# A tile of eight gate-norm weights that takes 64 bytes per partition in place of 32

## The chip, the cores and the metric

The kernel runs on one NeuronCore of one Trainium2 chip. The metric is the device time of one execution in microseconds (us). Matrix products run on TensorE (PE in the profile, its loads of stationary operands PEld), elementwise work on VectorE (DVE) and ScalarE (ACT), a little on GpSimd (POOL). All bulk transfers are issued from SyncE's queue (SPq).

## The reference

One block over 2048 tokens of width 1024, in float32, cut to what matters here:

```python
n = rms_norm(h, attn_norm)
z = n @ w_in                        # columns for two groups of heads
o_g = gated linear attention of 4 heads, chunked, from z
o_m = softmax attention of 8 heads with a block-causal mask, from z
h = h + concat(o_g, o_m) @ w_out
m = rms_norm(h, mlp_norm)
h = h + square(relu(m @ w_mlp_up)) @ w_mlp_down          # 1024 -> 4096 -> 1024
gate = sigmoid(rms_norm(h, ple_norm) @ w_ple_gate + b_ple_gate)
h = h + (p @ w_ple_proj) * gate
```

The result has to agree with float32 products, so every matrix product here is made of three passes over rounded parts.

## The kernel before

**Three passes.** `split` (lines 89 to 96) writes an operand as a high part (ACT, line 92 or 95) and a low part (DVE, line 93 or 96), both of the type fp32r. `mm3` (lines 98 to 101) multiplies high by high, high by low and low by high into one PSUM tile. Its first argument is the stationary operand, its second the moving one. The first two passes have the same stationary operand, yet each matmul comes with a weight load of its own.

**Stages.** First the projections, with gated linear attention and the preparation of the softmax heads woven in (lines 544 to 716). Then attention, head by head (lines 730 to 906). Then, in two halves `H` of 1024 tokens each, the out projection, the MLP and the gate, called the tail here (lines 908 to 1034).

**The tail.** Its weights come in tiles `w2_` of [128, 2, 512] fp32r: `wtile2` loads 128x512 float32 into `raw2` and splits it. `wr_` holds 12 such tiles, `rw` four `raw2`. The activations lie in `xT` (two buffers of [128, 2, 8, 512]) or in `a` (five of [128, 2, 512]). All products of the tail have a moving operand of 512 columns and a stationary one of 128x128:

- out projection (line 955): 2 halves x 2 column halves x 8 token tiles x 8 depth blocks x 3 = 768 matmuls, stationary `xT`, moving `w2_`;
- MLP up (line 983): 2 x 16 groups of 256 features x 4 x 8 x 3 = 3072, stationary `w2_`, moving `xT`;
- MLP down (line 997): 2 x 16 x 8 x 4 x 3 = 3072, stationary `a`, moving `w2_`;
- gate and its partner product (lines 1023 and 1027): 2 x 2 x 8 x (8 + 2) x 3 = 960, stationary `xT` or `a`, moving `w2_`.

Between them stand groups of transposes: `rows_T` normalizes 128 rows, and PE turns them (line 921, 32 calls of eight transposes in two groups of four); line 1011 turns `p` (16 pairs).

**The projections' counterpart.** In the first stage the weights are tiles `w`, the normalized rows `nT0` and `nT1`. Most products there move `w` (256, 304 or 320 columns) past a stationary `nT`; the GLA queries and keys (line 667 on) move 512 columns of `nT` past a stationary `w`.

**Where tiles lie.** Pools hand out bytes of each partition one after another, a tile in whole units of 32 bytes; pools marked `side="right"` grow from the other end. On the left, after the constants, stand `cc` (`gain_m` of 4096 bytes, `gain_p` of 32, `bias_p` of 4096, in this order), then `rw`, then `wr_`. Start addresses in the built program, in bytes of a partition:

| tile | start before | start after | mod 64 before | mod 64 after |
|---|---|---|---|---|
| `gain_p` | 22944 | 22944 | 32 | 32 |
| `bias_p` | 22976 | 23008 | 0 | 32 |
| `raw2` (4 buffers) | 27072 + 2048 i | 27104 + 2048 i | 0 | 32 |
| `w2_` (12 buffers) | 35264 + 4096 i | 35296 + 4096 i | 0 | 32 |
| `xT` (2) | 163808 + 32768 i | same | 32 | 32 |
| `a` (5) | 110560 + 4096 i | same | 32 | 32 |
| `w` (9, projections) | 163296 + 2560 i | same | 32 | 32 |
| `nT0`, `nT1` | 186336, 202720 | same | 32 | 32 |
| `kT` (2), `qT` (4), attention | 163552 + 16384 i, 212960 + 4096 i | same | 32 | 32 |

The slices that matmuls take of these tiles start at multiples of 64 bytes within them, low parts included. (`vv`, the values of attention, is the exception: its blocks are 520 bytes apart.) So the last columns hold for every operand of a product.

**Order.** Each engine works through its instructions in the order of the text; the tile framework adds the waits.

Of the kernel before, what the change touches and what calls it, by code (L numbers as in the profile page):

```python
# [11 lines left out]
F32 = mybir.dt.float32  # L12
# [10 lines left out]
P = 128  # L23
# [6 lines left out]
PLE = 256  # L30
# [18 lines left out]
def hymba_block(ctx, tc, x, p, positions, attn_norm, w_in, gla_gate_w2, gla_gate_b,  # L49
# [7 lines left out]
    x, p, out = x[0], p[0, 0], out[0]  # L57
# [31 lines left out]
    def split(hi, lo, src, gain=None):  # L89
        """src (times a gain per partition) as a sum of two numbers of 12 bits each."""  # L90
        if gain is None:
            A.copy(out=hi, in_=src)  # L92
            V.tensor_tensor(out=lo, in0=src, in1=hi, op=ALU.subtract)  # L93
        else:
            A.activation(hi, src, AF.Copy, scale=gain)  # L95
            V.scalar_tensor_tensor(out=lo, in0=src, scalar=gain, in1=hi, op0=ALU.mult, op1=ALU.subtract)  # L96
# [6 lines left out]
    def rstd_of(ss, n, shape):  # L103
        """(ss / n + eps) ** -0.5: a first guess from the exponent bits, then Newton."""
        v = small.tile(shape, F32, name="rs_v")
        V.tensor_scalar(out=v, in0=ss, scalar1=1.0 / n, scalar2=EPS, op0=ALU.mult, op1=ALU.add)
        y = small.tile(shape, F32, name="rs_y")
        A.activation(y, v.bitcast(I32), AF.Exp, bias=y0_b, scale=Y0_S)
        for _ in range(3):
            a = small.tile(shape, F32, name="rs_a")  # L110
            V.tensor_tensor(out=a, in0=y, in1=y, op=ALU.mult)  # L111
            V.scalar_tensor_tensor(out=a, in0=a, scalar=-0.5, in1=v, op0=ALU.mult, op1=ALU.mult)  # L112
            r = small.tile(shape, F32, name="rs_y")
            V.scalar_tensor_tensor(out=r, in0=a, scalar=1.5, in1=y, op0=ALU.add, op1=ALU.mult)
            y = r
        return y
# [12 lines left out]

    def gain_cols(pool, name, vec, n):  # L130
        g = pool.tile([P, n], F32, name=name)
        for k in range(n):
            dma(out=g[:, k:k + 1], in_=vec[k * P:(k + 1) * P].unsqueeze(1))
        return g

    # ================================================= projections, GLA, MLA heads
    pgl = ExitStack()
# [60 lines left out]
    rows = tmp([4, P], "rows")  # L198
# [46 lines left out]
    def rope_tables():  # L245
# [7 lines left out]
        for i in range(NF):  # L253
            f = float(np.float32(np.float64(THETA) ** (-(2.0 * i) / ROPE)))
            V.tensor_scalar(out=ang[:, :, i], in0=pos, scalar1=f, scalar2=None, op0=ALU.mult)
        # angles brought into [-pi, pi]: 2 pi in three parts
        MAGIC = 12582912.0
# [30 lines left out]

    # operands whose zeros stay: scores, queries and states kept apart by head
    st8, xq8, sz = [], [], []  # L290
# [18 lines left out]
    def later(f, n):  # L309
        """Run f when n more pieces have come."""  # L310
        if f is not None:
            rest.append(f)
        while len(rest) > n:
            rest.pop(0)()

    LL, LC, EB, DP = 1, 1, 2, 3

    # ---- GLA of one half block (two chunks of 128 tokens), in pieces
    def gla_pieces(u, tok0, gq, gk, bt, gvs, gss):
# [73 lines left out]
        def chunk(c):  # L393
# [15 lines left out]
            for g in range(2):  # L409
                for j in range(2):  # L410
                    js = slice(j * 64, j * 64 + 64)
                    V.scalar_tensor_tensor(out=new[js, g, j], in0=state[js, g, j], scalar=eb[js, g, c, P - 1:P],
                                           in1=pk[js, g], op0=ALU.mult, op1=ALU.add)
            # output norm and gate
            ss = small.tile([P, GH], F32, name="oss")
# [22 lines left out]

    # ---- MLA heads of one token tile, four heads at a time
    def mla_weights(c):  # L440
# [13 lines left out]
    def mla_tile(b, tt, c, wts, cT, krr, kss, rt, rc):  # L454
# [8 lines left out]
        for k in range(2):  # L463
# [6 lines left out]
        V.tensor_scalar(out=ssq[:, 0], in0=ssq[:, 0], scalar1=rc[:, 1, 0, tt:tt + 1], scalar2=None, op0=ALU.mult)  # L470
        # rotation of the query, its gains in the tables
        qa = ml.tile([P, 4, ROPE], F32, name="qa", bufs=1)
# [23 lines left out]
                        in1=rc[:, 0, :, tt:tt + 1].broadcast_to([P, 2, 4]), op=ALU.mult)  # L496
        # the gains of both sides go to the query
        for hh in range(4):
# [21 lines left out]

    pend = []          # pieces of the GLA of the block before
    mla_q = []         # token tiles of MLA heads

# [6 lines left out]

    stores = []        # their last parts, one tile behind

# [11 lines left out]
    for b in range(NB):  # L544
        # ---- normalized rows, transposed: two tiles of four feature blocks
        nT = [nTp.tile([P, 2, 4, BLK], F32R, name=f"nT{i}") for i in range(2)]
# [17 lines left out]
        if b == 0:  # L564
            rope_tables()
            gain_columns()
        # ---- c_q | g_low | k_r, token-major
        rt = []
# [15 lines left out]
        for tt in range(4):  # L584
# [11 lines left out]
            A.activation(sq[:, 0:ROPE], kr, AF.Square, accum_out=kss[:, tt:tt + 1])  # L596
            # rotary part of the shared key, its gains in the tables
            ra = small.tile([P, ROPE], F32, name="kra")
# [12 lines left out]

        # ---- log decays and their running sums in the chunks
        bts = []
# [19 lines left out]
        if b == 0:  # L633
            level_masks()
        # ---- c_kv and GLA values, token-major
        gvs = []
        wy = wtiles([(O_C + QR, KVR), (O_GV, 192)])
        for tt in range(4):
# [14 lines left out]
            drain(DY)  # L653
        # the norms of c_q and c_kv, left for the heads: r and r * r
        rc = ml.tile([P, 2, 2, 4], F32, name="rc")
# [9 lines left out]

        # ---- GLA queries and keys, feature-major
        gqk = []
# [17 lines left out]

        # ---- rest of the GLA values, token-major
        wz = wtiles([(O_GV + 192, 320)])
# [8 lines left out]

        # ---- GLA output gates, token-major: silu without its factor 1/2
        gss.extend(gin.tile([P, 2, GH * GV], F32, name="gs", bufs=GSB) for _ in range(2))
# [31 lines left out]

    # ================================================= attention, head by head
    pat = ExitStack()
# [11 lines left out]
    def shift_pieces(h, jb, kT):  # L744
        """The rows' maxima over their keys, negated, as one more row of the queries."""
        qT = ah.tile([QK + 1, 2, BLK], F32R, name="qT", bufs=4)
# [36 lines left out]
    def attend(h, jb, kT, vv, qT):  # L783
        npair = 2 * jb + 2
        # the blocks on the diagonal come first
        order = [npair - 2, npair - 1] + list(range(npair - 2))
# [59 lines left out]

    LOOK = 3           # pairs of key blocks whose scores run ahead
    AHEAD = 3          # steps whose maxima run ahead
    steps = [(h, jb) for h in range(MH) for jb in range(4)]
# [57 lines left out]

    # ================================================= out projection, MLP, PLE
    pcr = ctx.enter_context(ExitStack())
# [14 lines left out]
    for H in range(2):  # L924
        t0 = H * 1024
        # ---- h = x + mix @ w_out
        mix, hts = [], []
        for c in range(2):
            if c == 1 and H == 1:
                w_first = wout(0)  # L930
            m = xTp.tile([P, 2, 8, BLK], F32R, name="xT")
            for k in range(8):
                raw = rw.tile([P, 512], F32, name="raw2")
                dma(out=raw, in_=mixd[k, :, t0 + c * BLK:t0 + (c + 1) * BLK])
                split(m[:, 0, k], m[:, 1, k], raw)
            mix.append(m)
            if c == 0 and H == 0:
                gain_m = cc.tile([P, D], F32, name="gain_m")
                dma(out=gain_m, in_=mlp_norm[0].partition_broadcast(P))
                gain_p = gain_cols(cc, "gain_p", ple_norm[0], 8)  # L940
                bias_p = cc.tile([P, D], F32, name="bias_p")
                dma(out=bias_p, in_=b_ple_gate[0].partition_broadcast(P))
            for tt in range(c * 4, c * 4 + 4):
                ht = hp.tile([P, D], F32, name="h")
                dma(out=ht, in_=x[t0 + tt * P:t0 + (tt + 1) * P, :])
                hts.append(ht)
        for nh in range(2):
            ns = slice(nh * 512, (nh + 1) * 512)
            w = w_first if nh == 0 else wout(nh)
            for tt in range(8):  # L950
                ts_ = slice((tt % 4) * P, (tt % 4 + 1) * P)
                ps = ps_mm()
                m = mix[tt // 4]
                for k in range(8):
                    mm3(ps, (m[:, 0, k, ts_], m[:, 1, k, ts_]), (w[k][:, 0], w[k][:, 1]), k == 0, k == 7)
                V.tensor_tensor(out=hts[tt][:, ns], in0=ps, in1=hts[tt][:, ns], op=ALU.add)
                # the first rows' norms run beside the products of the others
                if nh == 1 and tt >= 4:
                    if tt == 4:
                        mT = [xTp.tile([P, 2, 8, BLK], F32R, name="xT")]  # L960
                    rows_T(hts[tt - 4], gain_m, mT[0], slice((tt - 4) * P, (tt - 3) * P))
        # ---- MLP
        mT.append(xTp.tile([P, 2, 8, BLK], F32R, name="xT"))
        late = [(hts[tt], gain_m, mT[1], slice((tt - 4) * P, (tt - 3) * P)) for tt in range(4, 8)]
        rT = []
        for fg in range(FF // 256):
# [24 lines left out]
            for tt in range(8):  # L991
# [8 lines left out]
                if fg == FF // 256 - 1:  # L1000
                    if tt % 4 == 0:
                        rT.append(xTp.tile([P, 2, 8, BLK], F32R, name="xT"))
                    rows_T(hts[tt], None, rT[tt // 4], slice((tt % 4) * P, (tt % 4 + 1) * P))
        # ---- PLE
        pT = [ap_.tile([P, 2, 512], F32R, name="a").rearrange("p l (k t) -> p l k t", k=2) for _ in range(4)]
# [58 lines left out]
```

## Time and profile before

| | |
|---|---|
| device time, median of 3 runs | 3169.53 us (3169.33 to 3169.77) |
| span of the profiled execution, first to last instruction | 3163.8 us |
| PE busy | 3037.9 us, 96% |
| PE loads of stationary operands | 2453.2 us, 78% |
| DVE busy | 1958.0 us, 62% |
| ACT busy | 1251.1 us, 40% |
| share of the DMA engines, main queue | 25.6% |

The profile gives the span of its execution and no other time of it; 5.7 us lie between that span and the median of the timed runs. The stages by the trace: projections to about 720 us, attention to 1268 us, the tail to the end.

Matmuls are pipelined: a row of the timeline gives the start of each and a modelled end, which overlaps the next start. The pace of a row of matmuls is therefore read from start to start, never from a mean duration. PEclk is the granted clock as a share of full speed (1.00 is the 2.4 GHz level, 0.5 the 1.2 GHz level). The trace leaves one trailing underscore out of a tile's name and keeps its number: `w__20209` is a buffer of `w2_`.

### The profile page before, as it was taken

Reading aid. Unit: us, or ns where it says so; the run is one execution under the profiler, and the core shown is the slowest. Engines: PE = TensorE matmul, PEld = TensorE weight load, DVE = VectorE, ACT = ScalarE, POOL = GpSimd, SP = SyncE. Lnnn points to the kernel's source line nnn. Section 1 sums busy time; section 2 is a strip of 40 time slices with the busy share of each in tenths; the row PEclk is TensorE's granted clock in tenths of the full one; section 3 lists DMA queues with packets and bytes.
Section 4 is the critical chain, followed back from the end, with each engine's and each line's share of the span. In section 5 each row is a group of like instructions: output and inputs, shape, how many; then the busy total and the mean of one; then the engine's idle time right before and its main releaser. Section 6 shows DMA issues by size and latency. Waiting matters only on the chain.

```text
span 3163.8 us, 41322 instructions
## 1 busy us (share of the span) xinstructions
PE 3037.9 (96%) x14851; PEld 2453.2 (78%) x14851; DVE 1958.0 (62%) x4389; ACT 1251.1 (40%) x2540; POOL 203.2 (6%) x408
## 2 busy tenths in 40 slices
PE   7899898979999999999999999999999999999999
PEld 6888887766677777778888888878878888888877
DVE  6979898887887886464444444464464444444463
ACT  7566665634666667332221222142232222212231
POOL 3322322220000000000000000000000000000000
PEclk9999999987999999999999999999999999999999
DMA  4535344361423220411111111114211111111111
GB/s 122 147 87 156 103 131 123 95 163 44 124 67 101 68 67 14 148 53 41 53 50 45 50 44 54 40 54 149 91 54 54 41 54 40 54 40 54 41 51 52
DMA packets 222525, 238.77 MB, mean 75 GB/s; under 512 B 26630, under 2 KB 174160, under 8 KB 220528
## 3 DMA queue, kind: packets, MB, share of 16 engines
q1 hardware_dynamic: 222000, 236.01, 25.6%
q8 instruction: 117, 1.92, 0.2%
q14 instruction: 88, 0.72, 0.1%
q0 software_dynamic: 320, 0.13, 0.0%
HBM read 185.60 MB, written 50.46 MB: 75 GB/s over the span
## 4 chain that ended last, share of the span: by engine, by line
PE 78%; DVE 13%; ACT 4%; issue 3%; DMA 1%; POOL 0%; SPq 0%; DVEq 0%; ACTq 0%; POOLq 0%
PE mm L101 11%; PE mm L100 11%; PE mm L99 11%; PE big L99 10%; PE big L100 9%; PE big L101 9%; PE mm L823 5%; PE tp L758 2%; PE big L797 2%; PE big L799 2%; PE big L798 2%; DVE w L96 2%; DVE rs_a L112 1%; DVE rs_a L111 1%; DVE qn L499 1%
## 5 line engine op out<-in xcount | busy, mean ns | idle before, releaser
L999 DVE TENSOR_TENSOR h<-big,h 128x1024 f32<-128x1024 f32 x256 | 313.2, 1223 | 280.8 <-PE big L101 279.7
L823 PE MATMUL mm<-ph,vv 128*66 128x512 f32 (+3 forms) x960 | 244.6, 368 | 2.9 <-ACT ph L92 2.2
L99 PE MATMUL mm<-w,nT 128*128 128x320 f32 (+2 forms) x640 | 204.4, 320 | 5.6 <-ACT w L95 2.6
L100 PE MATMUL mm<-w,nT 128*128 128x320 f32 (+2 forms) x640 | 199.5, 313 | 5.8 <-DVE w L96 5.3
L93 DVE TENSOR_TENSOR ph<-pe,ph 128x1024 fp32r<-128x1024 f32 (+4 forms) x224 | 176.6, 797 | 38.4 <-ACT ph L92 36.8
L101 PE MATMUL mm<-w,nT 128*128 128x320 f32 (+2 forms) x640 | 198.4, 311 | 1.7 <-DVE nT L93 1.7
L765 DVE TENSOR_REDUCE mx<-tp 128x1 f32<-128x512 f32 (+2 forms) x288 | 169.9, 607 | 15.4 <-PE tp L758 13.5
L823 PEld LDWEIGHTS mm<-ph,vv 128*66 128x66 f32 (+1 forms) x960 | 127.3, 139 | 55.5 <-ACT ph L92 3.2
L92 ACT CAST ph<-pe 128x1024 fp32r<-128x1024 f32 (+4 forms) x224 | 156.2, 712 | 28.7 <-PE mm L823 25.9
L99 PEld LDWEIGHTS mm<-w,nT 128*128 128x128 f32 x640 | 126.6, 198 | 11.0 <-ACT w L95 4.9
L100 PEld LDWEIGHTS mm<-w,nT 128*128 128x128 f32 x640 | 126.5, 198 | 9.1 <-DVE w L96 8.9
L758 PE MATMUL tp<-kT,qT 96*128 96x512 f32 (+2 forms) x320 | 128.1, 407 | 4.2 <-DVE mx L765 2.3
L101 PEld LDWEIGHTS mm<-w,nT 128*128 128x128 f32 x640 | 126.3, 197 | 4.3 <-DVE nT L93 2.4
L96 DVE SCALAR_TENSOR_TENSOR w<-raw,gain_a,w 128x256 fp32r<-128x256 f32 (+2 forms) x224 | 119.0, 544 | 10.0 <-ACT w L95 9.3
L797 PE MATMUL big<-qT,kT 97*128 97x512 f32 (+1 forms) x320 | 122.7, 383 | 1.2 <-ACT qT L778 0.3
L95 ACT ACTIVATE w<-raw,gain_a 128x256 fp32r<-128x256 f32 (+2 forms) x224 | 110.7, 533 | 29.7 <-DMA raw<-in_w_in_dram 14.6
L798 PE MATMUL big<-qT,kT 96*128 96x512 f32 (+1 forms) x320 | 120.3, 376 | 0.0
L799 PE MATMUL big<-qT,kT 96*128 96x512 f32 (+1 forms) x320 | 119.9, 375 | 0.0
L804 ACT ACTIVATE pe<-big 128x1024 f32<-128x1024 f32 x96 | 98.2, 1023 | 28.1 <-PE big L799 27.2
L758 PEld LDWEIGHTS tp<-kT,qT 96*128 96x128 f32 x320 | 62.4, 196 | 36.3 <-DVE mx L765 12.8
L810 ACT ACTIVATE pe<-big 128x512 f32<-128x512 f32 (+3 forms) x128 | 54.3, 436 | 67.4 <-DVE big L809 60.4
L1029 DVE TENSOR_TENSOR sg<-big,bias_p 128x512 f32<-128x512 f32 x32 | 22.1, 690 | 89.7 <-PE big L101 89.7
(3372 smaller groups left out, 8258.6 us busy)
## 6 DMA issues: line engine op xcount, KB each, us to landing
raw<-in_w_mlp_up_dram SPq DMA_DIRECT2D x128, 256.0 KB, 2.9
raw<-in_w_mlp_down_dram SPq DMA_DIRECT2D x128, 256.0 KB, 3.2
raw<-in_w_in_dram SPq DMA_DIRECT2D x160, 128.0 KB, 2.5
qd<-qko SPq DMA_DIRECT2D x64, 192.0 KB, 2.7
kd<-qko SPq DMA_DIRECT2D x64, 192.0 KB, 3.1
kT<-kd SPq DMA_DIRECT2D x8, 1536.0 KB, 11.6
qT<-qd SPq DMA_DIRECT2D x32, 384.0 KB, 4.3
vd<-vt SPq DMA_DIRECT2D x32, 260.0 KB, 3.4
```

The lines of the kernel that those rows point to most:

```text
L93: V.tensor_tensor(out=lo, in0=src, in1=hi, op=ALU.subtract)
L96: V.scalar_tensor_tensor(out=lo, in0=src, scalar=gain, in1=hi, op0=ALU.mult, op1=ALU.subtract)
L99: T.matmul(o, lhsT=a[0], rhs=b[0], start=first, stop=False)
L100: T.matmul(o, lhsT=a[0], rhs=b[1], start=False, stop=False)
L101: T.matmul(o, lhsT=a[1], rhs=b[0], start=False, stop=last)
L758: T.matmul(ps[:, :w_], lhsT=qT[0:QK, 0, s_ * P:(s_ + 1) * P], rhs=kT[0:QK, 0, c0:c0 + w_], start=True, stop=True)
L765: V.tensor_reduce(out=mx[:, a:a + 1], in_=ps[:, :w_], axis=AX.X, op=ALU.max)
L797: T.matmul(o, lhsT=kT[:, 0, ks], rhs=qT[:, 0, c0:], start=True, stop=False)
L798: T.matmul(o, lhsT=kT[0:QK, 0, ks], rhs=qT[0:QK, 1, c0:], start=False, stop=False)
L799: T.matmul(o, lhsT=kT[0:QK, 1, ks], rhs=qT[0:QK, 0, c0:], start=False, stop=True)
L823: T.matmul(po[0:vs.stop - vs.start, c0:], lhsT=vv[:, kb, vs], rhs=ph[:, l, e, c0:], start=(kb == 4 * jb and n_ == 0), stop=(lastk and n_ = ...
L999: V.tensor_tensor(out=hv, in0=ps, in1=hv, op=ALU.add)
```

## The change

`gain_cols` gets the width of its tile as an argument, and its one call asks for 16 columns, of which 8 are filled and read as before. All that lies behind `gain_p` on the left side (`bias_p`, `raw2`, `w2_`) starts 32 bytes further on. The number of instructions of each engine, their order, their shapes, the DMAs and the pools' buffer counts are the same in both programs. The rest of the change takes comments out.

```diff
@@ helper
-    def gain_cols(pool, name, vec, n):
-        g = pool.tile([P, n], F32, name=name)
+    def gain_cols(pool, name, vec, n, width):
+        g = pool.tile([P, width], F32, name=name)
         for k in range(n):
             dma(out=g[:, k:k + 1], in_=vec[k * P:(k + 1) * P].unsqueeze(1))
         return g
@@ first half of the out projection
-                gain_p = gain_cols(cc, "gain_p", ple_norm[0], 8)
+                gain_p = gain_cols(cc, "gain_p", ple_norm[0], 8, 16)
```

## Rows read from the trace of the kernel before

**Rows 1.** The page: busy time by engine; granted clock in 40 slices.
```profile
PE 3037.9 (96%) x14851; PEld 2453.2 (78%) x14851; DVE 1958.0 (62%) x4389; ACT 1251.1 (40%) x2540; POOL 203.2 (6%) x408
...
PEclk9999999987999999999999999999999999999999
```

**Rows 2.** By stretch (us): length, engines' busy time, clock, DMA share, GB/s.
```profile
1365.00:2070.00 705.00, 704.91 (x3038) 566.87 (x3037) 331.93 (x412) 160.46 (x268) 0.00 (x0) 1.00 0.16 48
2070.00:2112.00 42.00, 38.67 (x187) 30.49 (x186) 35.43 (x111) 20.30 (x43) 0.00 (x0) 0.92 0.11 32
2305.00:3015.00 710.00, 709.05 (x3058) 569.93 (x3057) 336.37 (x425) 164.35 (x276) 0.00 (x0) 1.00 0.16 49
```

**Rows 3.** The chain of waits from 1260 us to the end, shares by line.
```profile
by line: PE big L99 15.8%; PE big L100 15.8%; PE big L101 15.7%; PE mm L100 15.2%; PE mm L99 15.2%; PE mm L101 15.1%; DVE xT L93 1.2%; PE tp L921 0.8%; DVE nrm L125 0.4%; DMA raw<-mixd 0.4%; issue 0.4%; DVE rs_a L112 0.3%; DVE rs_y L114 0.3
```

**Rows 4.** PE's waits from 1268 us on: total us, how many, longest.
```profile
PE tp L921 <- DVE nrm L125: 5.0, 2, 2.5
PE mm L99 <- ACT xT L92: 1.8, 3, 0.8
PE tp L1011 <- DVE xT L93: 1.7, 3, 1.0
```

**Rows 5.** Line 99 alone from 1268 us on: length, PE busy, PEld busy, clock.
```profile
1268.00:3164.00 1896.00, 1040.12 (x2624) 493.37 (x2624) 1.00 0.19 59
```

**Rows 6.** Timeline of PE: start us, us, line, tiles; MLP up, then down.
```profile
2006.01 0.40 PE L99 MATMUL mm<-xT,w__20209 128*128 128x512 f32 x1
...
2017.21 0.40 PE L99 MATMUL big<-w__20229,a 128*128 128x512 f32 x1
...
2028.41 0.40 PE L99 MATMUL big<-w__20229,a 128*128 128x512 f32 x1
```

**Rows 7.** Timeline of PE: GLA queries, 512 columns of nT move, w stands.
```profile
71.09 0.39 PE L99 MATMUL mm<-nT,w 128*128 128x512 f32 x1
...
76.53 0.34 PE L99 MATMUL mm<-wu,cT 128*128 128x384 f32 x1
```

**Rows 8.** By stretch: that of rows 7, and one of attention (rows 11).
```profile
71.09:76.53 5.44, 5.44 (x25) 4.51 (x24) 3.24 (x7) 4.20 (x9) 0.00 (x0) 1.00 0.59 171
1235.07:1236.93 1.86, 1.86 (x9) 1.51 (x8) 1.15 (x2) 1.86 (x4) 0.00 (x0) 1.00 0.00 0
```

**Rows 9.** Timeline of PE: the same products after a pause, second block.
```profile
239.80 0.39 PE L100 MATMUL mm<-nT,w 128*128 128x512 f32 x1
...
241.19 0.39 PE L100 MATMUL mm<-nT,w 128*128 128x512 f32 x1
...
244.59 0.39 PE L100 MATMUL mm<-nT,w 128*128 128x512 f32 x1
```

**Rows 10.** Timeline of PE: w moves past nT, 320 columns, then 256.
```profile
282.24 0.30 PE L100 MATMUL mm<-w,nT 128*128 128x320 f32 x1
...
285.76 0.31 PE L100 MATMUL mm<-w,nT 128*128 128x320 f32 x1
...
303.45 0.28 PE L101 MATMUL mm<-w,nT 128*128 128x256 f32 x1
...
304.53 0.28 PE L99 MATMUL mm<-w,nT 128*128 128x256 f32 x1
```

**Rows 11.** Timeline of PE: scores of attention, qT moves past kT.
```profile
1235.07 0.40 PE L799 MATMUL big<-qT,kT 96*128 96x512 f32 x1
...
1236.93 0.40 PE L798 MATMUL big<-qT,kT 96*128 96x512 f32 x1
```

**Rows 12.** Timelines of ACT and DVE in the MLP: splits of w2_ and a.
```profile
1500.11 0.62 ACT L92 CAST w__17449<-raw 128x512 fp32r<-128x512 f32 x1 [18.26 <-PE big L101]
...
1509.23 0.62 ACT L92 CAST a<-rl__17236 128x512 fp32r<-128x512 f32 x1 [0.76 <-DVE rl__17236 L987]
...
1500.76 0.69 DVE L93 TENSOR_TENSOR w__17449<-raw,w__17449 128x512 fp32r<-128x512 f32 x1
...
1509.88 0.69 DVE L93 TENSOR_TENSOR a<-rl__17236,a 128x512 fp32r<-128x512 f32 x1 [0.69 <-ACT a L92]
```

## The prediction

> **What bounds the kernel now.** I read the page's busy times first: PE is busy 96% of the span, no other engine over 62%, and its clock is at the full level in nearly every slice [rows 1]. The change touches only tiles of the tail, so next come the tail's stretches: in the 705 us from 1365 us on PE is busy 704.91 us, in the 710 us of the second half's MLP 709.05 us, always at clock 1.00, with DVE under half busy and the DMA engines at 0.16 [rows 2]. The chain of waits shows the same from the other side: over the last 1904 us the six product groups hold 15.8 + 15.8 + 15.7 + 15.2 + 15.2 + 15.1 = 92.8% [rows 3], and PE's largest waits there add up to a few us [rows 4]. So the tail lasts as long as its matmuls take, and the question is their pace alone.
>
> **The pace, and where it differs.** The reader should divide differences of starts. MLP up: 48 matmuls from 2006.01 to 2017.21 us, 233.3 ns each. MLP down: 48 from 2017.21 to 2028.41 us, 233.3 ns [rows 6]. At 2.4 GHz 512 columns take 213.3 ns; the matmul costs 560 cycles, 48 more than it has columns. In the projections the same kind of product, 512 columns past 128x128, with the same three passes, runs at (76.53 - 71.09) / 24 = 226.7 ns, which is 544 cycles [rows 7]. That stretch has the same clock of 1.00, more DMA (0.59 of the engines against 0.16) and busier ACT [rows 2, 8], so a quieter neighbourhood does not explain the faster pace. In the table of start addresses one difference stands out: there both operands start at 32 mod 64, in the tail one starts at 0 and its partner at 32, in either role. The change makes the tail's pairs 32 and 32. I take the pace of [rows 7] for them.
>
> **The change part by part.**
>
> *Instructions.* None is added, removed or moved. The eight small loads of `gain_p` stay, the 32 added bytes are never read.
>
> *DVE and ACT.* The splits into `w2_` now read and write at 32 mod 64. The tail already has both kinds: into `w2_`, starts at 0, ACT takes 0.62 us and DVE 0.69 us; into `a`, starts at 32, 0.62 and 0.69 us [rows 12]. Cost nothing. `bias_p` is read by 32 sums of DVE, the same kind of instruction; nothing either.
>
> *DMAs.* Same packets, to starts 32 bytes on. A slower landing isn't shown; rows of before bound it, since transfers into 32 mod 64 tiles (`w`'s raw tiles) feed a stage that runs at 0.59 of the DMA engines [rows 8], over three times the MLP's 0.16 [rows 2]. Nothing, hidden behind 44.8 us of products per feature group (192 x 233.3 ns).
>
> *Matmuls.* Line 99 has 2624 matmuls in the tail [rows 5], lines 100 and 101 as many: 7872, as the loops say. If each takes 226.7 in place of 233.3 ns, 6.67 ns less, that is 52.5 us: the upper bound. On the path are 0.928 x 1904 us = 1767 us of them [rows 3], 7573 matmuls: 50.5 us. The rest stands in the stretches where DVE's norms set the pace, such as 2070 to 2112 us, with PE busy 38.67 of 42 us [rows 2]; a faster PE only waits there.
>
> *Settling.* The fast pace is not there at once. After a pause the projections' products need a few matmuls: from 239.80 to 241.19 us six take 231.7 ns each, the next fifteen 226.7 ns [rows 9]. In the tail 32 calls of `rows_T` and 16 pairs of line 1011 put transposes into the row of products, and there are some waits: about 60 breaks, an estimate from the loops and the waits [rows 4]. Six to nine matmuls at +5 ns after each are 1.8 to 2.7 us; I take 2.3 us.
>
> *Sum.* -50.5 + 2.3 = -48.2 us. The profiled span of 3163.8 us becomes 3115.6 us. With the 5.7 us that lie between it and the median, and nothing in them to change, the median comes to 3121.5 us. Bounds of this case: 52.5 us at most, and 42 us if the breaks double or the start of a stage hides more; 3117 to 3127.5 us.
>
> **A rule against it.** The rows show two paces at one clock [rows 6 to 8]. The Trainium skill's page "TensorE: Matmul & The Clock Gate", section "Back-to-back issue gap", gives one for 512 columns, 518 cycles warm, with no word on addresses; its page "SBUF — State Buffer", section "Who interferes with whom", says that the moving operand and the weight load have independent read ports and that PE waits on no one. By these two the start address could not matter and the time would stay at 3169.5 us. The trace disagrees with the figure: no row of products here is at 518 cycles, but at 544 or 560. On the ports it decides nothing, so this stays a rival.
>
> **The rivals.**
>
> *A second cause (no change).* The pace of rows 7 could belong to something else that the two stages don't share, for instance how far apart the tiles lie. For it: in attention `qT` and `kT` both start at 32 mod 64, and yet eight matmuls from 1235.07 to 1236.93 us take 232.5 ns each at clock 1.00 [rows 8, 11]. Against it: those use 96 or 97 of 128 rows, and in attention products of other tiles and widths come every few matmuls, so they may never settle (six were needed in [rows 9]); and `w` moving past `nT` also runs at columns + 32 cycles, 146.7 ns for 320 columns and 120.0 ns for 256 [rows 10]. Time: 3169.5 us.
>
> *One role only.* Rows 7 have the `w2_`-like tile standing and 512 columns of activations moving: MLP up exactly. For the other 4800 matmuls, where `w2_` moves, rows 10 show the pace at 256 and 320 columns only. If only up gains: 3072 x 6.67 ns x 0.96 (the share on the path, 7573 / 7872) = 19.7 us, less a third of the settling, 18.9 us: 3150.6 us. If only the others gain: 30.7 - 1.5 = 29.2 us: 3140 us.
>
> *Slower.* If moving `w2_` from 32 mod 64 costs what it now costs to have unlike partners, and comes on top, those 4800 matmuls go to 576 cycles, 240.0 ns: +30.7 us, while up gains 18.9 us: +12 us, 3181.5 us. It decides from 237.4 ns for these matmuls on (18.9 us over 0.96 x 4800 is 4.1 ns). For it: the 512-column moving weight has no twin in the trace. Against it: up moves `xT` from 32 mod 64 and down moves `w2_` from 0, and both run at 233.3 ns [rows 6], so the start of the moving operand by itself costs nothing; and rows 10.
>
> **How the numbers follow.** Main case 0.69; one role 0.12; no change 0.12; slower 0.07. The prediction is the main case's 3121.5 us. Main case and one role hold 0.81, from 3117 us (widened to 3115, for a settling shorter than I took and the runs' own spread) to 3150.6 us, so the range is 3115 to 3151 us. A measurement of this kernel can tell about 0.2%, 6.3 us, from no change: both gaining cases are faster by more (0.81), the second cause is within it (0.12), the slower case beyond it (0.07).
>
> **What would show it.** In the profile after: starts in MLP up and down 226.7 ns apart in place of 233.3, 48 in 10.88 us; if only one of the two is so, the second rival holds; if both are at 233.3, the start mod 64 was not the cause. The share of PE stays near 96% and the span loses what the tail loses; attention and projections keep their times, 1268 us together. DVE's 0.69 us and ACT's 0.62 us per split stay. After transposes the first products should run some ns slower and then settle. The prediction is wrong if the pace in the MLP settles anywhere but at 544 cycles, or if PE's waits on splits or loads grow by more than a few us, for then the gain is given back to a wait.

## The result, and the profile after

The changed kernel takes 3114.82 us, median of four runs (3113.32 to 3121.36), against 3169.43 us of the kernel before beside it (3165.17 to 3169.77). The ratio is 0.9834, with a 95% interval from 0.9820 to 0.9848. Run again later with another four (experiment e8), it took 3120.5 us, 0.9852 [0.9837, 0.9867] of the kernel before. The profiled execution after took 3113.97 us, with a span of 3112.0 us.

The page of the changed kernel: busy time by engine, and the granted clock in 40 slices.

```profile
PE 2982.2 (96%) x14851; PEld 2449.3 (79%) x14851; DVE 1954.9 (63%) x4389; ACT 1251.7 (40%) x2540; POOL 202.9 (7%) x408
...
PEclk9999999998999999999999999999999999999999
```

The counts of instructions are those of [rows 1]. PE's busy time fell by 55.7 us and the span by 51.8 us; DVE and ACT work about as long as before (1954.9 and 1251.7 us), and PE's granted clock is at the full level in nearly all slices of both pages. The shares look unchanged, because the bounding engine and the span shrank together.

The stretches that answer to [rows 2], in the same columns: MLP of the first half, the norms behind it, MLP of the second half.

```profile
1361.00:2045.00 684.00, 683.91 (x3031) 566.05 (x3032) 329.81 (x406) 160.14 (x268) 0.00 (x0) 1.00 0.16 50
2045.00:2086.00 41.00, 37.09 (x190) 29.43 (x189) 36.77 (x116) 21.10 (x44) 0.00 (x0) 0.99 0.08 27
2276.00:2964.00 688.00, 687.02 (x3048) 568.14 (x3047) 333.31 (x415) 162.94 (x273) 0.00 (x0) 1.00 0.16 51
```

PE is as full as before, at clock 1.00 again. Nearly the same number of instructions now takes 21 us less in the first stretch and 22 us less in the second. The short stretch between them, where DVE's norms set the pace, is about as long as it was.

PE's timeline in the MLP after, which answers to [rows 6]: the first row begins MLP up, the second MLP down, the third what follows.

```profile
1898.08 0.39 PE L99 MATMUL mm<-xT,w__19657 128*128 128x512 f32 x1
...
1908.96 0.39 PE L99 MATMUL big<-w__19677,a 128*128 128x512 f32 x1
...
1919.84 0.39 PE L99 MATMUL big<-w__19677,a 128*128 128x512 f32 x1
```

Both groups of 48 take 10.88 us, so 226.7 ns each: 544 cycles, the pace of [rows 7], in both roles of the weight tile.

The chain of waits from 1260 us to the end, shares by line, then PE's largest waits from the end of attention on (total us, how many, longest), answering to [rows 3, 4].

```profile
by line: PE big L99 15.5%; PE big L100 15.4%; PE big L101 15.4%; PE mm L100 15.3%; PE mm L101 15.2%; PE mm L99 15.2%; DVE xT L93 1.3%; PE tp L921 0.7%; DVE nrm L125 0.6%; DVE h L999 0.5%; issue 0.5%; DVE rs_y L114 0.4%; DVE rs_a L112 0.4%; 
```

```profile
PE tp L921 <- DVE nrm L125: 5.0, 2, 2.5
PE tp L1011 <- DVE xT L93: 1.9, 2, 1.0
PE mm L99 <- ACT xT L92: 1.9, 3, 0.9
PE big L99 <- DVE sg L1031: 1.1, 2, 0.6
```

The six product groups still hold 92.0% of the chain, and no wait has grown by more than a fraction of a us. The gain was not given back to a split or a load.

### The profile page after: what moved, and what is told of

It reads as the page before. It is cut to its first block, busy times and chain, and to the rows that moved or that the text cites. A ratio compares the mean times of both kernels' runs of the same rounds, so it can differ in the third digit from the quotient of the medians.

```text
span 3112.0 us, 41322 instructions
## 1 busy us (share of the span) xinstructions
PE 2982.2 (96%) x14851; PEld 2449.3 (79%) x14851; DVE 1954.9 (63%) x4389; ACT 1251.7 (40%) x2540; POOL 202.9 (7%) x408
## 4 chain that ended last, share of the span: by engine, by line
PE 77%; DVE 15%; ACT 3%; issue 3%; DMA 2%; POOL 0%; SPq 0%; DVEq 0%; ACTq 0%; POOLq 0%
PE mm L101 10%; PE mm L100 10%; PE mm L99 10%; PE big L99 9%; PE big L100 9%; PE big L101 9%; PE mm L823 5%; PE tp L758 2%; PE big L797 2%; PE big L799 2%; PE big L798 2%; DVE w L96 2%; DVE rs_a L112 1%; DVE rs_a L111 1%; DVE rs_y L114 1%
## 5 line engine op out<-in xcount | busy, mean ns | idle before, releaser
L797 PEld LDWEIGHTS big<-qT,kT 97*128 97x128 f32 x320 | 61.1, 191 | 21.6 <-ACT pe L810 6.7
```

The source lines that it names most:

```text
L797: T.matmul(o, lhsT=kT[:, 0, ks], rhs=qT[:, 0, c0:], start=True, stop=False)
```

## The experiments

In all texts "up" is the group where `xT` moves past the standing weight tile, "down" the one where the weight tile moves past an `a` (the partner product of the gate is counted here), and the third group (out projection and gate) moves the weight tile past `xT`. A pace is the mean distance of starts over all products of 512 columns in the tail, without pauses. Kernels with one run stand against one run of the kernel before beside them: 3172.5 us for e1 to e4, 3165.26 us for e5, e7, e9 and e10, 3168.09 us for e13.

**The table that sorts them.** The start of `w2_` less the start of its partners, mod 256 bytes, and the paces:

| kernel | difference mod 256 | up, ns | down, ns | third, ns | time, us |
|---|---|---|---|---|---|
| before | 224 | 233.3 | 233.3 | 233.3 | 3169.43 |
| after | 0 | 226.76 | 226.77 | 227.03 | 3114.82 |
| e1 | 0, all at 192 mod 256 | 226.76 | 226.77 | 227.06 | 3119.78 |
| e2 | 0; with `a` 32 | 226.88 | 233.24 | 227.93 | 3144.49 |
| e3 | 64 | 233.30 | 230.97 | 228.97 | 3156.38 |
| e4 | 0; mod 512 it is 256 | 226.74 | 226.77 | 227.03 | 3122.76 |
| e5 | 16, 80, 144, 208 in turn | 231.76 | 232.78 | 232.50 | 3163.48 |
| e7 | 128 | 233.25 | 233.17 | 232.41 | 3168.21 |
| e13 | 16 | 233.01 | 231.67 | 231.65 | 3162.13 |

In up the weight tile stands and in the other groups it moves. So the role and the sign of the difference change together, and where the groups of one kernel differ (e3, e13), no run tells which of the two makes it.

**e1: alike at another place.** Is it likeness, or the place of 32? The kernel before, with 32 bytes put in front of the right-hand pools, so that all three start at 0 mod 64.

```
+     padp = rpool("padp", 1, pcr)
+     V.memset(padp.tile([P, 8], F32, name="pad"), 0.0)
      xTp = rpool("xTp", 2, pcr)
```

> The kernel before with 32 bytes put in front of the right-hand tiles of the tail, so that w2_, xT and a all start at 0 mod 64. Theory 'relation' (a product runs at columns + 32 cycles when its two operands start alike mod 64, at columns + 48 when they don't): MLP up and down at 226.7 ns from start to start, span near that of the changed kernel, 3112 us. Theory 'place' (32 mod 64 is the good start for w2_): 233.3 ns, span near 3164 us.

PE's timeline of e1, MLP up, down and what follows:

```profile
1903.98 0.39 PE L99 MATMUL mm<-xT,w__19662 128*128 128x512 f32 x1
...
1914.86 0.39 PE L99 MATMUL big<-w__19682,a 128*128 128x512 f32 x1
...
1925.74 0.39 PE L99 MATMUL big<-w__19682,a 128*128 128x512 f32 x1
```

Again 10.88 us for each 48. The whole gain comes without touching `gain_p` or `w2_`: the relation counts, not the place.

**e2: one partner unlike.** The changed kernel, with the same 32 bytes in front of the pool of `a` alone.

```
+     padp = rpool("padp", 1, pcr)
+     V.memset(padp.tile([P, 8], F32, name="pad"), 0.0)
      ap_ = ...
```

> The changed kernel with the tiles a moved to 0 mod 64; w2_ and xT stay at 32. 'Relation': MLP up (w2_ and xT) stays at 226.7 ns, MLP down and the partner product of the gate (a and w2_), 3072 + 192 matmuls, go back to 233.3 ns, +21 us, span 3133 us. 'Place' (of w2_ alone): nothing moves, 3112 us. If the pace is one of the whole stage rather than of each product, up changes too.

PE's timeline of e2, the same three places:

```profile
1913.58 0.39 PE L99 MATMUL mm<-xT,w__19662 128*128 128x512 f32 x1
...
1924.46 0.39 PE L99 MATMUL big<-w__19682,a 128*128 128x512 f32 x1
...
1935.66 0.39 PE L99 MATMUL big<-w__19682,a 128*128 128x512 f32 x1
```

Up stays at 10.88 us for 48, down is back at 11.20 us, 233.3 ns. The pace belongs to each product and its own two operands, not to the stage. The span of e2's profile, 3142.7 us, is 24.8 us above that of e1 (3117.9 us) on the same occasion, where 21 us were expected; the gate's products, whose rows stand between those of the slow partner product, lose a little as well (third group 227.93 ns).

**e3 and e4: how far must the likeness go?** `gain_p` takes 128 bytes in e3 and 320 in e4. In e3 `w2_` is like its partners mod 64 but not mod 128; in e4 it is like them mod 256 but not mod 512.

```
-                gain_p = gain_cols(cc, "gain_p", ple_norm[0], 8, 16)
+                gain_p = gain_cols(cc, "gain_p", ple_norm[0], 8, 32)     # e4: 80
```

> The changed kernel with gain_p of 32 columns: w2_ starts at 32 mod 64 like its partners, but at 32 mod 128 where they start at 96. 'Relation mod 64': 226.7 ns, 3112 us. 'Relation mod 128 or more': 233.3 ns, 3164 us.

> The changed kernel with gain_p of 80 columns: w2_ starts alike with its partners mod 256, but 256 bytes off mod 512, as kT and qT of attention do, which run at 232.5 ns. 'Relation mod 64': 226.7 ns, 3112 us. 'Relation mod 512', which would explain attention's pace too: 233.3 ns, 3164 us.

PE's timeline of e3, then of e4, the same three places:

```profile
1916.34 0.40 PE L99 MATMUL mm<-xT,w__19657 128*128 128x512 f32 x1
...
1927.54 0.40 PE L99 MATMUL big<-w__19677,a 128*128 128x512 f32 x1
...
1938.54 0.39 PE L99 MATMUL big<-w__19677,a 128*128 128x512 f32 x1
```

```profile
1906.06 0.39 PE L99 MATMUL mm<-xT,w__19657 128*128 128x512 f32 x1
...
1916.93 0.39 PE L99 MATMUL big<-w__19677,a 128*128 128x512 f32 x1
...
1927.81 0.39 PE L99 MATMUL big<-w__19677,a 128*128 128x512 f32 x1
```

In e3 up is as slow as in the kernel before (11.20 us) and down stands between the paces (11.00 us, 229.2 ns). Likeness mod 64 is therefore not what makes the pace. In e4 both are fast (10.87 and 10.88 us): nothing beyond mod 256 is needed.

**e5, e13 and e7: smaller and larger distances.** In e5 the used part of `w2_` begins 16 bytes into a tile of 4160 bytes. That was a slip: 4160 is no multiple of 256, so the pool's twelve places stand at distances of 16, 80, 144 and 208 in turn. e13 takes 4352 bytes, so that all stand at 16. In e7 `gain_p` takes 192 bytes, which leaves the pairs alike mod 128 alone.

```
-  t_ = wr_.tile([P, 2, 512], F32R, name="w2_")
+  t_ = wr_.tile([P, 1040], F32R, name="w2_")[:, 4:1028].rearrange("p (l n) -> p l n", l=2)   # e5
+  t_ = wr_.tile([P, 1088], F32R, name="w2_")[:, 4:1028].rearrange("p (l n) -> p l n", l=2)   # e13
+  gain_p = gain_cols(cc, "gain_p", ple_norm[0], 8, 48)                                       # e7
```

> The changed kernel with each w2_ started 16 bytes into a longer tile: 48 mod 64 against its partners' 32. 'Unlike by any amount is slow': 233.3 ns in MLP up and down, span near 3164 us. 'Only the 32-byte half counts' (16 bytes is within the same half): 226.7 ns, 3112 us.

> The changed kernel with gain_p of 48 columns: w2_ starts at 96 mod 256 where its partners start at 224; alike mod 128. 'Relation mod 128' (as the run that was alike mod 64 alone suggests, 233.3 ns in MLP up): 226.7 ns, 3112 to 3120 us. 'Relation mod 256': 231 to 233 ns, 3150 to 3164 us.

> Experiment e5 began the weight tile's used part 16 bytes into a tile of 4160 bytes, so that its twelve places did not stand at one distance from their partners but at 16, 80, 144 and 208 mod 256 in turn; within one group of MLP up its four weight tiles ran at 228.3, 232.5, 235.0 and 232.5 ns. Here each tile takes 4352 bytes (a multiple of 256), so every place stands 16 bytes past likeness mod 256. Theory, only equal starts mod 256 give the quick pace: no product settles at 226.7 ns, MLP up and down at 228 to 234 ns, time 3128 to 3168 us, and all four weight tiles of a group at one pace. Rival, nearness is enough (the distance counts only from 32 bytes on): 226.7 to 227.1 ns everywhere and the changed kernel's time, 3113 to 3124 us.

PE's timeline of e7, the same three places; then that of e13, where the first row begins MLP up of 96 products, the second down and the third is its 49th product:

```profile
1919.84 0.40 PE L99 MATMUL mm<-xT,w__19657 128*128 128x512 f32 x1
...
1931.04 0.40 PE L99 MATMUL big<-w__19677,a 128*128 128x512 f32 x1
...
1942.23 0.40 PE L99 MATMUL big<-w__19677,a 128*128 128x512 f32 x1
```

```profile
1906.77 0.39 PE L99 MATMUL mm<-xT,w__19657 128*128 128x512 f32 x1
...
1929.16 0.39 PE L99 MATMUL big<-w__19677,a 128*128 128x512 f32 x1
...
1940.29 0.39 PE L99 MATMUL big<-w__19677,a 128*128 128x512 f32 x1
```

Both are slow in both groups: 233.3 and 233.1 ns in e7, 233.2 and 231.9 ns in e13. The time of e7 is no shorter than that of the kernel before beside it. In e5 each of the four distances gives between 230.1 and 233.8 ns on average. Of the distances tried, 0 mod 256 alone gives 226.7 ns; even 16 bytes lose most of the gain.

**e9: attention's scores over 128 rows.** `kT` and `qT` are alike mod 256 in the kernel before too (both at 224), yet run at 232.5 ns [rows 11]. The changed kernel, with both tiles filled with zeros to 128 rows, so that no product uses 96 or 97.

```
-  kT = ah.tile([QK + 1, 2, S], F32R, name="kT")
+  kT = ah.tile([P, 2, S], F32R, name="kT")
+  G.memset(kT[QK:].bitcast(F32), 0.0)          # qT likewise
-  T.matmul(o, lhsT=kT[0:QK, 0, ks], rhs=qT[0:QK, 1, c0:], start=False, stop=False)
+  T.matmul(o, lhsT=kT[:, 0, ks], rhs=qT[:, 1, c0:], start=False, stop=False)
```

> The changed kernel with kT and qT filled up to 128 rows by zeros that GpSimd writes, and the second and third pass of the scores taken over all 128 rows. 'Fewer rows keep attention's scores from the fast pace': 226.7 ns for qT past kT in place of 233.4, some 1000 matmuls, span 6 us shorter, 3106 us. 'They never settle, whatever their rows' (products of other tiles come between): 233 ns, span 3112 us or a little more.

PE's timeline of one row of scores in the changed kernel, then of the same row in e9:

```profile
1233.66 0.39 PE L798 MATMUL big<-qT,kT 96*128 96x512 f32 x1
...
1235.29 0.40 PE L799 MATMUL big<-qT,kT 96*128 96x512 f32 x1
...
1235.99 0.40 PE L799 MATMUL big<-qT,kT 96*128 96x512 f32 x1
```

```profile
1235.90 0.40 PE L800 MATMUL big<-qT,kT 128*128 128x512 f32 x1
...
1237.52 0.39 PE L801 MATMUL big<-qT,kT 128*128 128x512 f32 x1
...
1238.20 0.39 PE L801 MATMUL big<-qT,kT 128*128 128x512 f32 x1
```

With 96 and 97 rows seven products take 232.9 ns each and the three behind them 233.3. With 128 rows the first seven take 231.4 ns and the last three 226.7. So these scores can settle once they have all 128 rows; in this row they need about seven products for it. It is the only row of scores of that length in the trace, but shorter ones go the same way: the fourth product of a row takes 229.2 ns on average in e9 and 233.9 in the changed kernel (36 rows each). Most rows are cut off by transposes and value products before they settle: over the whole stage the pace went only from 233.3 to 232.2 ns, and the time (3118.2 us) lies within the changed kernel's own, 3113.32 to 3124.27 us. e9 also ends the turn of 97 and 96 rows from product to product; whether that or the missing rows kept the pace slow, it doesn't part.

**e10, e11, e12: attention's value products.** Is more to be had where `ph` moves past `vv`? In e10 a key block's values take 640 bytes and `ph` starts 64 bytes later, alike mod 128; in e11 768 bytes, with the low part 512 bytes in, alike mod 256; e12 is e11 with e9.

```
-  vv = ah.tile([P, NT, VW], F32R, name="vv")
+  vv = ah.tile([P, NT, VS], F32R, name="vv")           # e11: VS, VL = 192, 128
+  padw.append(aw.tile([P, 16], F32, name="padw", bufs=1))
-  ops = [(slice(0, MV + 2), 0), (slice(MV + 2, VW), 0), (slice(0, MV + 2), 1)]
+  ops = [(slice(0, MV + 2), 0), (slice(VL, VS), 0), (slice(0, MV + 2), 1)]
```

> The changed kernel with the values of attention in blocks of 640 bytes, the low part 384 bytes behind the high one, and ph moved by 64 bytes, so that every pair of ph and vv starts alike mod 128 (before: blocks of 520 bytes, any start). 'Relation mod 128' with settling: ph past vv comes from 232 to 227 to 229 ns, 552 counted matmuls and some 950 in all, 3 to 5 us off the span. 'Never settles': 232 ns, no change; the loads of vv carry 23% more bytes.

> The changed kernel with the values of attention, vv, in blocks of 768 bytes, the low part 512 bytes behind the high one, and ph moved by 64 bytes: every pair of ph and vv alike mod 256 (blocks and low parts come by a DMA each). 'Relation mod 256, for 64 and 66 stationary columns too': ph past vv goes from 232 to 227 to 229 ns, about 950 matmuls, 3 to 5 us faster than the changed kernel. 'Attention's rows are too short to settle': 232 ns, no change.

> The same, and kT and qT filled to 128 rows by zeros from GpSimd, so that all large products of attention are alike mod 256 and use all rows. 'Fewer rows and unlike neighbours keep attention from settling': both qT past kT and ph past vv near 227 ns, some 2000 matmuls x 5 to 6 ns, 8 to 12 us faster than the changed kernel. 'Pauses keep it from settling': 231 to 233 ns and no gain, or a loss where GpSimd's zeros are waited for.

None gains. The pace of `ph` past `vv` is 232.1 ns in the changed kernel, 232.4 in e10, 233.2 in e11 and 232.7 in e12, although e11 has the likeness that suffices in the tail. The times are 3123.02 us (one run), 3121.38 (3121.14 to 3122.89) and 3124.45 us (3121.77 to 3125.83). Where e11's values were expected to settle, that was a miss. Short rows are not the whole cause: the last row of attention has 24 value products one behind the other. PE's timeline of it in the changed kernel, in e11 and in e12, the last two with starts alike mod 256:

```profile
1259.51 5.73 PE L823 MATMUL mm<-ph,vv 128*66 128x512 f32 x24
```

```profile
1265.79 5.71 PE L830 MATMUL mm<-ph,vv 128*66 128x512 f32 x24
```

```profile
1267.44 5.80 PE L832 MATMUL mm<-ph,vv 128*66 128x512 f32 x24
```

At 226.7 ns from start to start they would take some 5.6 us. What else differs from the tail, weights of 66 or 64 columns in place of 128 and the turn between the two, was not tried apart, so the cause stays open.

**e8: the changed kernel again**, without an edit, beside e11 and e12.

> The changed kernel as it is, timed beside the next two. 3112 to 3122 us.

It took 3120.5 us (3116.31 to 3124.27), so e11 and e12 are no faster than it, and no kernel that was run is shown to beat the changed one. Its paces in the tail are 226.76, 226.77 and 227.05 ns, those of the first profile.

## Why the prediction was right, and where its reason was not

**What bounds the kernel: right.** The tail shrank by what its products shrank. From the last value product of attention to the end it took 1897.8 us before and 1847.1 us after, 50.7 us less; projections and attention together went from 1266.0 to 1264.8 us. The chain of waits shows the end of attention 1.2 us earlier after the change, with the same load of 3.3 us on the way into the tail. The end of attention before, then after (start us, us, what):

```profile
1260.83 5.58 PE mm L823 x24
...
1268.30 3.33 DMA raw<-mixd
```

```profile
1259.67 5.58 PE mm L823 x24
...
1267.14 3.30 DMA raw<-mixd
```

**The pace of 226.7 ns in every role: right.** Up and down both stand at 544 cycles, as forecast, so "one role only" falls, and so does "slower": the moving weight at 32 mod 64 costs nothing.

**The reason, start mod 64: wrong, and harmless by luck.** This is the step that failed: "there both operands start at 32 mod 64, in the tail one starts at 0 and its partner at 32". What counts is whether the two starts are alike mod 256. Mod 256 the start of `w2_` went from 192 to 224, and `xT`, `a`, and the projections' `w` and `nT` (of [rows 7, 10]) all start at 224. The long rows that the prediction compared, the tail's and those of `w` and `nT`, held no pair that is alike mod 64 but not mod 256, so they could not tell the two rules apart, and a table of starts mod 64 read as well as one mod 256 would have. But the kernel before did hold such a pair, outside the table of starts. `cT` starts at 107168, `wu` at 124768 and `wkv` at 130912: all at 32 mod 64, yet `wu` and `wkv` 192 past `cT` mod 256. PE's timeline of the kernel before, six products of 384 columns and the next of 512:

```profile
76.53 0.34 PE L99 MATMUL mm<-wu,cT 128*128 128x384 f32 x1
...
77.58 0.39 PE L99 MATMUL mm<-wkv,cT 128*128 128x512 f32 x1
...
78.05 0.40 PE L101 MATMUL mm<-wkv,cT 128*128 128x512 f32 x1
```

The six take about 175 ns each, some 35 cycles over their columns, but the first two of `wkv` take about 234 ns each, where the rule mod 64 gives 226.7. With nine products at a time this was a warning and no more. By the prediction's rule e3 and e7 would have run like the changed kernel, near 3115 to 3120 us; they took 3156.38 and 3168.21 us. The 64 bytes that the tile takes are right since they move `w2_` by 32; 128 or 192 bytes, alike mod 64 just as well, lose most of the gain or all of it.

**The second cause: a part of it was there.** This rival's example, "how far apart the tiles lie", is near to what counts, if the distance is taken mod 256; its forecast of no change failed because the change brings that distance to 0. The prediction explained away `kT` and `qT`, alike and yet slow [rows 11], by their 96 and 97 rows or their short rows. e9 bears that out: with 128 rows the end of a long row reaches 226.7 ns, and few rows are long enough to profit.

**Splits, DMAs: right.** The splits into `w2_` after the change, ACT's and DVE's, as in [rows 12]:

```profile
1514.26 0.61 ACT L92 CAST w__17469<-raw 128x512 fp32r<-128x512 f32 x1
```

```profile
1495.02 0.69 DVE L93 TENSOR_TENSOR w__17454<-raw,w__17454 128x512 fp32r<-128x512 f32 x1
```

**The Trainium skill on this.** Its page "TensorE: Matmul & The Clock Gate", section "Back-to-back issue gap", gives 518 cycles for 512 columns as the gap of a matmul by itself, and about 131 ns for each of a stream in which every matmul has a weight load, as here. After the change the tail stands at 544 cycles, 226.7 ns, so the trace agrees with neither. Its page "SBUF — State Buffer", section "Who interferes with whom", gives the moving operand and the weight load independent ports; e1 and e2 show that the two starts together set the pace all the same. Whether a port is the reason, no run here shows.

**Settling: right in kind, too large.** The timeline of PE where transposes end and the gate's products begin, after:

```profile
2072.02 1.03 PE L921 MATMUL tp<-ident,nrm 128*128 128x128 f32 x8
2072.81 0.49 PE L99 MATMUL big<-w__21132,xT 128*128 128x512 f32 x1
2073.13 0.40 PE L100 MATMUL big<-w__21132,xT 128*128 128x512 f32 x1
...
2074.53 0.39 PE L100 MATMUL big<-w__21142,xT 128*128 128x512 f32 x1
...
2075.22 0.39 PE L100 MATMUL big<-w__21147,xT 128*128 128x512 f32 x1
```

Six products take 233.3 ns each and the next three 230, much as the first six in [rows 9]; then transposes cut the row off. But over the tail the excess over 226.67 ns is only 0.09, 0.10 and 0.36 ns per product in the three groups, some 1.1 us over the 7800 or so that could be counted, where I took 2.3 us. The trace shows about 45 rows that begin behind transposes or other work, where I took 60 breaks, and 1.1 us over 45 is 25 ns for each, where I took 38. And of the 52.5 us of the upper bound less this 1.1, nearly all arrived (50.7 of 51.4), where I had left 2 us off the path.

**The size.** Forecast 3121.5 us, measured 3114.82, 6.7 us less. Of these, 3.7 us are the term "5.7 us between span and median": it set a profile beside the median of other executions, while the profiled execution after lies 2.0 us above its span, and that of every experiment 1.7 to 2.1 us. Another 2.5 us are the tail (50.7 for 48.2), 1.2 us the stages ahead of it, which the change doesn't touch; 0.2 us is a slip in my sum (3115.6 + 5.7 is 3121.3), and the median lies 0.85 us above the profiled execution. The time fell 0.18 us under the lower end of the range. With e8's median of 3120.5 us, the miss is no larger than what the same kernel shows between two occasions.

## What to carry to other kernels

Before a table of addresses is read as a rule, ask which other moduli would sort the same rows the same way, and whether the table holds every operand of a product; two kernels that move one tile by 64 or 128 bytes settle it. Where a long row of `fp32r` products runs at columns + 48 cycles at full clock with PE never waiting, compare the starts of each product's two operands mod 256 bytes, product by product, since a pad of a few bytes in front of one pool may be the whole cure. A span and a median may be added only if both come from the same execution.

## What the runs showed that was not expected

- `fp32r` products of 512 columns past 128x128 weights settle at columns + 32 cycles (226.7 ns) when the starts of their two operands are alike mod 256 bytes. They stay near columns + 48 (232.4 to 233.3 ns) at distances of 32, 128 and 224; 16 gave 231.7 to 233.0 ns. At a distance of 64 the standing role of the weight tile was slow (233.3) and its moving role between (231.0 and 229.0 ns on average).
- Scores over 96 and 97 rows stay at 233 ns for a whole row of products in which 128 rows reach 226.7 ns, at starts alike mod 256 in both.
- Value products with 66 or 64 columns of weights don't settle at 226.7 ns within a row of 24, though their starts are alike mod 256 (e11, e12).
- Why the relation of two starts costs 16 cycles per product is not settled: no run here separates the weight load's reading from the moving operand's.
